# Delta rule on Trainium2: one cyclic list of pieces orders all engines, decay matrices and output weight parts come from the first stage

## The chip, the cores and the metric

The kernel runs on one core of one Trainium2 chip. The metric is the device time of one execution in microseconds (us); the figure for a kernel is the median of its runs. The engines are named as in the profile: PE is TensorE, DVE is VectorE, ACT is ScalarE, POOL is GpSimd, SP is SyncE, which here only issues transfers (DMAs). Each engine works through its own queue in order; a DMA queue on SP or ACT does so too.

## The reference

One inference step of a two-layer encoder over 2048 prompt tokens and 32 sample tokens. Layer one is a gated delta rule with 8 heads of 128, layer two is banded attention. What matters here is the first layer:

```python
def delta_layer(x, conv_buf, s0, w_in, conv_w, a_log, dt_bias, norm_w, w_out, ln_g, ln_b):
    proj = x @ w_in
    qkv, new_buf = causal_conv(proj[..., :CONV_DIM], conv_buf, conv_w)
    z = proj[..., CONV_DIM:CONV_DIM + A_VW].reshape(b, l, A_HEADS, A_DV)
    ...
    o, s_new = gated_delta_rule(q, k, v, g, beta, s0.astype(jnp.float32))
    o = o * lax.rsqrt(jnp.mean(o * o, -1, keepdims=True) + RMS_EPS) * norm_w * jax.nn.silu(z.astype(jnp.float32))
    out = o.reshape(b, l, A_VW).astype(x.dtype) @ w_out
    return layer_norm(DN_ALPHA * x + out, ln_g, ln_b), new_buf, s_new.astype(x.dtype)
```

and within the delta rule, for each chunk of tokens:

```python
    gcum = jnp.cumsum(gb, axis=-1)
    decay = jnp.exp(jnp.where(incl, gcum[..., :, None] - gcum[..., None, :], -jnp.inf))
    lower = jnp.where(strict, jnp.einsum('bhik,bhjk->bhij', kbeta, kc) * decay, 0.0)
    tmat = lower + jnp.eye(c, dtype=lower.dtype)
    ...
    intra = jnp.einsum('bhik,bhjk->bhij', qc, kc) * decay
    def step(s, xs):
        v_new = ui - jnp.einsum('bhck,bhkv->bhcv', wi, s)
        o = jnp.einsum('bhck,bhkv->bhcv', qd, s) + jnp.einsum('bhij,bhjv->bhiv', ai, v_new)
        s = s * gl[..., None, None] + jnp.einsum('bhck,bhcv->bhkv', kd, v_new)
        return s, o
```

The matrix `decay` depends on the gates alone, not on q, k, v or the state.

## The kernel before

All products that have a weight as an operand are made of fp32r parts: a weight or an activation is split into a high and a low part, and three matmuls (high-high, low-high, high-low) stand for one (`project`, lines 73 to 81).

Stage 1 (`P1.qkv`) takes 24 rows of q, k and v; each row is 5 blocks of 416 tokens of 24 matmuls. ACT copies a block from PSUM to the row tile `R` (L227), ACT and DVE do the convolution (L194, L196), the SiLU (L199, L200) and the squares. Ahead of the rows `gates` makes the cumulated log gates and writes one row tile `g_row` per 128 tokens to the DRAM scratch `gcum` (L379 to L382). Through rows 15 to 22 `split_out_weights` (L1031 to L1034) splits the first four of the eight slices of the output weight into parts and stores them in scratch `wo`. Then the gate projection z of the first blocks runs, with the block inverses of the first two chunks beside it (`Ahead`).

The delta stage (`Delta.run`) goes over 17 chunks: chunk 0 is the sample (32 tokens), chunks 1 to 16 have 128 tokens. For a chunk, `decays` adds the causal mask to the broadcast gates (one DVE addition of 128x1024, L542) and takes eight exponentials on ACT (L547); the result is `E`. `powers` takes two more exponentials of the gates (L638). `lower` multiplies k by k (`g`, L562) and then by E (L563); a 25-step chain on POOL (L585, L588) and 6 steps on DVE invert the 32-blocks of the triangle, small matmuls (L680 to L704) join them to 128. `errors` (ks, L714), `changes` (vp, L725), `seen` (op, L739 and L743) and `advance` (sp L755, state Sp L761) are the recurrence; `squares`, `norms`, `scale` (L787) and `emit` (otr L798, L799) are the output norm and gate.

The order of PE, DVE and ACT in this stage is the program's own: `run` advances generators of several chunks in turn by calls of `go`, and between them fills PE from one of two `Filler`s. The first holds 16 blocks of the gate projection (`late_z`) until cycle `OPEN` = 11; the second holds the output projection of finished tiles (po, L1089 to L1091), used from the last cycles on. SP and POOL are ordered by a scheduler. At cycle 11 the output projection's pool is opened; `load_part_weights` (L1036 to L1066) brings in the four split slices and splits the other four from raw: casts on ACT (L1059), subtractions on DVE (L1063), the fetches on the DMA queue of ACT (L1050, L1051), one step at a time as `side(True)` is called.

E has one buffer, the gates `gb` two, k two, q five.

Of the kernel before, what the change touches and what calls it, by code (L numbers as in the profile page):

```python
# [95 lines left out]
class P1:  # L96
# [49 lines left out]
    def qkv(self):  # L146
# [30 lines left out]
        parts = one.tile([128, 8, NT // 32], F32, tag="parts", name="parts")  # L177
        wo = split_out_weights(nc, one, "th", I["a_w_out"], T["wo"])
        for i in range(24):
# [34 lines left out]
        nc.sync.dma_start(self.O["conv"][:, :, :], self.convo[:])  # L214

# [71 lines left out]
    def late_z(self, pool, w, raw):  # L287


        nc = self.nc  # L290
        self.sub = nc.vector
        raws = [raw]

        def last(h, b, p, th):
            z = pool.tile([128, TB], F32, tag="z", name="z")
            nc.vector.tensor_scalar(out=z[:], in0=p[:, :TB], scalar1=self.nwh[:, 0:1], scalar2=None, op0=ALU.mult)
            nc.vector.scalar_tensor_tensor(out=z[:], in0=th[:], scalar=1.0, in1=z[:], op0=ALU.add, op1=ALU.mult)
            self.keep_gate(h, b, z)

        todo = None  # L300
        for h in range(8):
            self.fetched = raws.pop(0) if h < 7 else None
            if h < 6:
                raws.append(self.late_raw(pool, h + 2))
            for b in (3, 4):
                p = self.left_ps()
                for us in project(nc, p[:, :TB], w, self.x[b]):
                    yield us
                    if todo:
                        last(*todo)  # L310
                        todo = None
                th = pool.tile([128, TB], F32, tag="zth", name="zth")
                nc.scalar.activation(th[:], p[:, :TB], AF.Tanh, scale=0.5)
                todo = h, b, p, th
            self.split()
            w = self.next
        yield 0.0
        last(*todo)

# [7 lines left out]
def gates(nc, I, T, G, abT, gtmp, one, pt):  # L327
# [129 lines left out]
class Chunk:  # L457
    def __init__(self, t0, n):
        self.t0, self.n, self.ti, self.ready, self.pool = t0, n, t0 // 128, False, None
        self.split = 25  # L460


class Delta:

    OPEN = 11
    BUFS = 2

# [29 lines left out]
    def constants(self):  # L500
        nc, one = self.nc, self.one
        self.nm = one.tile([128, 128], F32, tag="nm", name="nm")
        nc.sync.dma_start(self.nm[:], self.I["nm"])
        self.tinit = one.tile([128, 32, 8], F32, tag="tinit", name="tinit")
        nc.sync.dma_start(self.tinit[:], self.I["tinit"])

    @staticmethod
    def bc(ap, n, w=128):
        return ap.unsqueeze(2).to_broadcast([n, 4, w])

    def load(self, ch, name, halves=(0, 1)):
        nc, T, n, ti = self.nc, self.T, ch.n, ch.ti
        own = ch.pool is not None and name != "z"
        w = n if own else 128
        if name in ("gb", "k") and 0 in halves:
            if own:
                ch.__dict__[name] = ch.pool.tile([128, 8, w], F32, tag="c" + name, name=name, bufs=1)
            else:
                ch.__dict__[name] = self.four.tile([128, 8, w], F32, tag=name, name=name, bufs=self.BUFS)
        for q in halves:  # L520
            hs = slice(q * 4, q * 4 + 4)
            if name in "vzq":
                src = T[name][ti, :, hs, :n]
# [6 lines left out]
                ch.__dict__.setdefault(name, []).append(t)  # L530
                nc.sync.dma_start(t[:, :, :n], src)
        if name == "gb":
            nc.sync.dma_start(ch.gb[:, :, :n], T["gcum"][ti, :, :n].partition_broadcast(128))
        if name == "k":
            nc.sync.dma_start(ch.k[:, :, :n], T["k"][ti, :, :, :n])

    def decays(self, ch):

        nc, V, G = self.nc, self.nc.vector, self.G
        n, ti = ch.n, ch.ti  # L540
        ch.E = self.two.tile([128, 8, 128], F32, tag="E", name="E", bufs=1)
        V.tensor_tensor(out=ch.E[:n, :, :n], in0=ch.gb[:n, :, :n],  # L542
                        in1=self.nm[:n, :n].unsqueeze(1).to_broadcast([n, 8, n]), op=ALU.add)
        yield
        for h in range(8):
            E = ch.E[:n, h, :n]
            nc.scalar.activation(E, E, AF.Exp, bias=G["ngc"][:n, ti, h:h + 1])  # L547
            if h % 4 == 3:
                yield

    def lower(self, ch):

        nc, V = self.nc, self.nc.vector
        n = ch.n
        ch.npr = self.two.tile([128, 8, 128], F32, tag="npr", name="npr")
        nb = self.sml.tile([128, 8, 32], F32, tag="nb", name="nb")
        for q in range(2):
            hs = slice(q * 4, q * 4 + 4)
            g = self.pa.tile([128, 4, 128], F32, tag="tr", name="g")
            for j in range(4):  # L560
                kt = ch.k[:, q * 4 + j, :n]
                nc.tensor.matmul(g[:n, j, :n], kt, kt, start=True, stop=True)  # L562
            V.tensor_tensor(out=ch.npr[:n, hs, :n], in0=g[:n, :, :n], in1=ch.E[:n, hs, :n], op=ALU.mult)  # L563
            yield
        for b in range(n // 32):
            bs = slice(32 * b, 32 * b + 32)
            nc.scalar.copy(nb[bs], ch.npr[bs, :, bs])
        ch.L = self.two.tile([128, 32, 32], F32, tag="L", name="L")
        ch.Tt = self.keep.tile([128, 32, 8], F32, tag="Tt", name="Tt")
        nc.scalar.copy(ch.Tt[:n], self.tinit[:n])  # L570
        yield
        V.transpose(ch.L[:n], nb[:n].rearrange("q p i -> q i p").unsqueeze(2).to_broadcast([n, 32, 4, 8]))
        yield

    def chain(self, ch, P, a, z):

        if ch.ready:
            return
        n, L, Tt = ch.n, ch.L, ch.Tt
        k = a // 8 * 8  # L580
        tm = self.sml.tile([128, 32 - k, 8], F32, tag="ta" if k else "tm", name="tm")
        for j in range(a, z):
# [4 lines left out]
            yield  # L587
# [3 lines left out]
    def turn_k(self, ch):  # L591
        nc, G, n = self.nc, self.G, ch.n
        ch.kd = []
        for q in range(2):
            kd = self.four.tile([128, 4, 128], F32, tag="kd", name="kd")
            tr = self.pa.tile([128, 4, 128], F32, tag="tr", name="tr")
            for j in range(4):
# [66 lines left out]
    def invert(self, ch):  # L664

        nc, V = self.nc, self.nc.vector
        if ch.n == 32:
            return
# [134 lines left out]
    def run(self, chunks, S, first, second, side, done):  # L803
# [44 lines left out]
        for i in range(len(chunks) + 1):  # L848
# [17 lines left out]
            if last:  # L866
                done(last)
# [997 lines left out]
```

## Time and profile before

| | us |
|---|---|
| median of 3 runs | 2196.88 (2190.58 to 2197.76) |
| the profiled execution | 2196.05 |
| its span | 2194.3 |
| PE busy | 2149.0 |
| DVE busy | 1373.7 |
| ACT busy | 917.6 |
| POOL busy | 841.7 |
| mean granted PE clock | 0.991 of full speed |

A row of a timeline is: start, duration, engine, line, operation, output<-inputs, shape, number of instructions joined in the row, and in brackets how long the engine had been idle before and what released it. A row of the windows is: the stretch, its length, then for each engine busy time and number of instructions, the granted PE clock, the share of the DMA engines that was busy, and GB/s. A group of instructions ends with its busy time and the mean duration of one in ns. Matmuls overlap in the pipeline, so that the duration of one is longer than its share of the time; the distance of starts is what counts. Stage 1 lies at about 0 to 600 us, the z stage and the inverses to about 692, the delta stage to about 1160; the rest is the end of the first layer's projection and the attention layer.

### The profile page before, as it was taken

To read this page: it belongs to the slowest core of one execution; us is meant where nothing else is said; L and a number is where in the kernel's file an instruction comes from. 1 tells how busy PE (TensorE), PEld (TensorE's weight loads), DVE (VectorE), ACT (ScalarE), POOL (GpSimd) and SP (SyncE) were. 2 spreads that over 40 slices of the span, in tenths; PEclk is the share of its full clock that TensorE was granted. 3 is DMA by queue.
4 is the path that set the end of the run, shared out by engine and by line. 5 is a ranking of instruction groups with operands and counts; after the bars stand their busy time and mean duration, and the time that the engine had idled before them with its cause. 6 is when DMAs were issued, how large, how long until landed. Compare 5 with 4: busy or idle time off the path is not lost.

```text
span 2194.3 us, 36636 instructions
## 1 busy us (share of the span) xinstructions
PE 2149.0 (98%) x13706; PEld 1982.3 (90%) x13706; DVE 1373.7 (63%) x2696; ACT 917.6 (42%) x2303; POOL 841.7 (38%) x1189
## 2 busy tenths in 40 slices
PE   8999999999999999999999999999999999999998
PEld 6999999999999899998888788999999987778885
DVE  3676666754466688888868876135442236668775
ACT  4444344433323677778741213222112235445442
POOL 1422212222211377888820201046441124556564
PEclk9999999999999999999999999999999999999999
DMA  5222222233355344446536754374221288233321
GB/s 198 68 60 79 68 78 68 91 117 97 97 152 156 100 139 148 128 134 216 191 98 198 239 186 154 100 235 167 70 76 67 86 181 267 78 96 97 103 67 53
DMA packets 250674, 274.48 MB, mean 125 GB/s; under 512 B 76112, under 2 KB 195216, under 8 KB 250224
## 3 DMA queue, kind: packets, MB, share of 16 engines
q1 hardware_dynamic: 240528, 256.97, 38.0%
q10 hardware_dynamic: 9968, 15.17, 2.1%
q8 instruction: 108, 1.77, 0.3%
q14 instruction: 70, 0.57, 0.1%
HBM read 168.53 MB, written 103.92 MB: 124 GB/s over the span
## 4 chain that ended last, share of the span: by engine, by line
PE 91%; POOL 3%; DMA 2%; DVE 1%; ACT 1%; issue 1%; ACTq 0%; SPq 0%; DVEq 0%; POOLq 0%
PE ps L77 17%; PE ps L79 17%; PE ps L78 17%; PE po L1089 5%; PE po L1091 5%; PE po L1090 5%; PE ot L1581 4%; PE S L1560 2%; PE tr L1575 2%; POOL Tt L588 1%; POOL tm L585 1%; PE g L562 1%; PE vp L725 1%; PE ks L714 1%; PE op L739 1%; PE gq L629 1%
## 5 line engine op out<-in xcount | busy, mean ns | idle before, releaser
L77 PE MATMUL ps<-act_hi,w_hi 128*128 128x416 f32 x2000 | 706.6, 354 | 4.5 <-ACT w_hi L53 3.2
L79 PE MATMUL ps<-act_hi,w_lo 128*128 128x416 f32 x2000 | 704.9, 353 | 2.0 <-POOL w_lo L54 1.2
L78 PE MATMUL ps<-act_lo,w_hi 128*128 128x416 f32 x2000 | 701.6, 351 | 0.0
L77 PEld LDWEIGHTS ps<-act_hi,w_hi 128*128 128x128 f32 x2000 | 377.0, 189 | 9.1 <-ACT w_hi L53 3.7
L79 PEld LDWEIGHTS ps<-act_hi,w_lo 128*128 128x128 f32 x2000 | 376.1, 188 | 6.8 <-POOL w_lo L54 1.7
L78 PEld LDWEIGHTS ps<-act_lo,w_hi 128*128 128x128 f32 x2000 | 376.5, 188 | 4.7 <-DVE act_lo L69 0.4
L54 POOL TENSOR_TENSOR w_lo<-w_raw,w_hi 128x1024 fp32r<-128x1024 f32 x44 | 117.6, 2673 | 469.2 <-ACT w_hi L53 443.1
L196 DVE SCALAR_TENSOR_TENSOR y<-R,convw,y 128x2083 f32<-128x2083 f32 x72 | 173.7, 2414 | 109.6 <-ACT y L194 74.1
L585 POOL TENSOR_TENSOR tm<-L,Tt 128x60 f32<-128x60 f32 (+19 forms) x373 | 139.4, 374 | 89.9 <-ACT vn L771 49.7
L588 POOL TENSOR_TENSOR Tt<-Tt,tm 128x60 f32<-128x60 f32 (+19 forms) x373 | 157.1, 421 | 29.2
L1568 POOL TENSOR_TENSOR P<-P,sm 128x384 f32<-128x384 f32 (+2 forms) x128 | 100.5, 806 | 172.9 <-DVE sm L1446 104.4
L227 ACT COPY R<-ps 128x416 f32<-128x416 f32 (+1 forms) x144 | 61.2, 448 | 199.0 <-PE ps L79 178.4
L1442 ACT ACTIVATE P<-S,nm 128x192 f32<-128x192 f32 (+3 forms) x260 | 104.6, 418 | 90.0 <-DVE nm L1435 43.3
L1089 PE MATMUL po<-wo_hi,g_hi 128*128 128x512 f32 x256 | 104.0, 406 | 1.8 <-ACT hT L1196 1.8
L1286 POOL TENSOR_TENSOR rs<-rs,sin 128x416 f32<-128x416 f32 x50 | 71.0, 1421 | 78.7 <-DVE rs L1285 72.2
L1091 PE MATMUL po<-wo_hi,g_lo 128*128 128x512 f32 x256 | 100.5, 393 | 0.0
L1090 PE MATMUL po<-wo_lo,g_hi 128*128 128x512 f32 x256 | 100.4, 392 | 0.0
L1581 PE MATMUL ot<-pt,vd 128*128 128x256 f32 x372 | 97.1, 387 | 1.6 <-ACT pt L1577 1.1
L53 ACT CAST w_hi<-w_raw 128x1024 fp32r<-128x1024 f32 x48 | 50.4, 1050 | 114.7 <-PE ps L78 87.3
L1089 PE MATMUL po<-wo,g_hi 128*128 128x512 f32 x224 | 92.9, 415 | 0.0
L1091 PE MATMUL po<-wo,g_lo 128*128 128x512 f32 x224 | 90.0, 402 | 0.0
L1090 PE MATMUL po<-wo,g_hi 128*128 128x512 f32 x224 | 89.8, 401 | 0.0
(306 smaller groups left out, 4041.2 us busy)
## 6 DMA issues: line engine op xcount, KB each, us to landing
w_raw<-in_w_in SPq DMA_DIRECT2D x40, 512.0 KB
w_raw<-in_b_w_in SPq DMA_DIRECT2D x20, 512.0 KB
gb<-s_gcum SPq DMA_DIRECT2D x17, 512.0 KB
k<-s_k SPq DMA_DIRECT2D x17, 512.0 KB
s_bz<-za SPq DMA_DIRECT2D x40, 208.0 KB
s_bq<-ra SPq DMA_DIRECT2D x40, 208.0 KB
s_q<-y SPq DMA_DIRECT2D x8, 1024.0 KB
s_k<-y SPq DMA_DIRECT2D x8, 1024.0 KB
```

The costliest lines, as they stand in the source:

```text
L54: sub.tensor_tensor(out=lo[:], in0=raw[:], in1=hi[:], op=ALU.subtract)
L77: nc.tensor.matmul(ps, hi[:, k, :], xh[:, k, :], start=(k == 0), stop=False)
L78: nc.tensor.matmul(ps, hi[:, k, :], xl[:, k, :], start=False, stop=False)
L79: nc.tensor.matmul(ps, lo[:, k, :], xh[:, k, :], start=False, stop=(k == KC - 1))
L196: nc.vector.scalar_tensor_tensor(out=y[:], in0=R[:, j:j + W], scalar=self.convw[:, i, j:j + 1], in1=y[:], op0=ALU.mult, op1=ALU.add)
L585: P.tensor_tensor(out=tm[:n, i0 - k:, :w], in0=L[:n, i0:, j:j + 1].to_broadcast(sh), in1=Tt[:n, j:j + 1, :w].to_broadcast(sh), op=ALU.mult)
L588: P.tensor_tensor(out=Tt[:n, i0:, :w], in0=Tt[:n, i0:, :w], in1=tm[:n, i0 - k:, :w], op=ALU.subtract)
L1089: nc.tensor.matmul(ps[:n], ghi[:, k, :n], w[0][:, k, cs], start=a, stop=False)
L1090: nc.tensor.matmul(ps[:n], ghi[:, k, :n], w[1][:, k, cs], start=False, stop=False)
L1091: nc.tensor.matmul(ps[:n], glo[:, k, :n], w[0][:, k, cs], start=False, stop=z)
L1442: nc.scalar.activation(P[u], src, AF.Exp, bias=nm[:, u:u + 1], scale=1.0, accum_out=sm[:, u:u + 1])
L1581: nc.tensor.matmul(ot[:, p], self.vd[:, kc0 + j, p, :], pt[:, 2 * j:2 * j + 2, :], start=(j == 0), stop=(j == nj - 1))
```

## The change

Four things change.

First, the decay matrices of all chunks are made in stage 1. `gates` also writes the exponentials of the cumulated gates (scratch `grow`), and 34 half tiles of E are made and stored in scratch `E` during rows 16 to 23. The delta stage loads E and grow ready-made.

```diff
+            if i >= 16:
+                for _ in range(5 if i < 18 else 4):
+                    next(matrices)
...
+    def decays(self):
+        nc, G, T = self.nc, self.G, self.T
+        nm = self.one.tile([128, 128], F32, tag="triu", name="nm")
+        nc.sync.dma_start(nm[:], self.I["nm"])
+        todo = [(t, q) for t in (NTT - 1, *range(NTT - 1)) for q in range(2)]
+        def load(m):
+            t, q = todo[m]
+            n, hs = min(128, NT - t * 128), slice(q * 4, q * 4 + 4)
+            E = self.one.tile([128, 4, 128], F32, tag=("parts", "sel", "gtmp")[m % 3], name="E")
+            nc.sync.dma_start(E[:, :, :n], T["gcum"][t, hs, :n].partition_broadcast(128))
+            return E, t, n, hs
+        ahead = [load(0), load(1)]
+        for m in range(len(todo)):
+            E, t, n, hs = ahead.pop(0)
+            if m + 2 < len(todo):
+                ahead.append(load(m + 2))
+            nc.vector.tensor_tensor(out=E[:n, :, :n], in0=E[:n, :, :n],
+                                    in1=nm[:n, :n].unsqueeze(1).to_broadcast([n, 4, n]), op=ALU.add)
+            for j in range(4):
+                h = hs.start + j
+                nc.scalar.activation(E[:n, j, :n], E[:n, j, :n], AF.Exp, bias=G["ngc"][:n, t, h:h + 1])
+            nc.scalar.dma_start(T["E"][t, :n, hs, :n], E[:n, :, :n])
+            yield
...
-        row = one.tile([H, 128], F32, tag="g_row", name="g_row", bufs=2)
-        V.tensor_copy(row[:, :n], tp[:H, :n])
-        nc.scalar.dma_start(T["gcum"][t, :, :n], row[:, :n])
+        row = one.tile([H, 2, 128], F32, tag="g_row", name="g_row", bufs=1)
+        V.tensor_copy(row[:, 0, :n], tp[:H, :n])
+        nc.scalar.activation(row[:, 1, :n], tp[:H, :n], AF.Exp)
+        nc.scalar.dma_start(T["gcum"][t, :, :n], row[:, 0, :n])
+        nc.scalar.dma_start(T["grow"][t, :, :n], row[:, 1, :n])
```

Second, all eight slices of the output weight are split in stage 1 (rows 7 to 22), and the delta stage loads the parts, 16 loads of 512 KB on SP, with no cast or subtraction left.

```diff
-            if 15 <= i < 23:
+            if 7 <= i < 23:
                 next(wo)
...
+def load_whole_weights(nc, pool, kept):
+    hi, lo = (pool.tile([128, KC, D], F32R, tag=n, name=n) for n in ("wo_hi", "wo_lo"))
     yield hi, lo
+    for k in range(KC):
+        nc.sync.dma_start(hi[:, k, :].bitcast(F32), kept[0, k])
+        nc.sync.dma_start(lo[:, k, :].bitcast(F32), kept[1, k])
         yield
```

Third, the order of the delta stage is one cyclic list. A piece `name+off` in cycle i is done for chunk i + off; names stand for the functions of before, cut into pieces for one engine each (G products of k by k, N their weighting, PC0 to PC5 the chain on POOL, T1 to T3 its end on DVE, v1 to v5 the joins, SU the state update, L.. loads, R the root, OSC the scaling, z and st the gating and its store).

```diff
+    OPEN = 11
+    FIRST = -5
+    WHOLE = 2
+    SPLIT = 25
+    ORDER = """
+        ta2+0 fq1+1 os0+0 v5+0 Lk+2 PC2+1 OSC+-1 Lq1+2 PC3+1 fq0+1 vn0+1 G0+2 u3+0 N0+2 G1+2 TT+2 otr0+-1
+        otr1+-1 N1+2 GA1+1 z0+-1 NB+2 tk0+1 tk1+1 vp0+0 vs0+0 PC4+1 kd0+1 st0+-1 z1+-1 Lv1+1 GA3+0 fk+1 L+2
+        PC5+1 kd1+1 vp1+0 Lv0+2 st1+-1 T1+1 oa0+0 T2+1 sp0+0 T3+1 tv1+1 SPR1+1 PC0+2 LE+3 o0+0 vs1+0 SU0+0 gq1+2
+        PC1+2 SPR2+1 os1+0 sp1+0 vn1+1 Lz0+0 oa1+0 SU1+0 sq0+0 at1+2 v1+1 Lgb+2 WH+1 gq0+2 at0+2 o1+0 y1+1 ks0+1
+        e0+1 U32+1 ks1+1 v2+1 v3+1 GA2+1 gth+0 sq1+0 WL+1 X+0 Lz1+0 Lq0+3 ta1+1 v4+1 gz1+0 tv0+2 GA0+2 u1+1 e1+1
+        R+0 gz2+0
+"""
...
+        gate.plan(order, self.FIRST + 2, self.WHOLE)
+        gate.begin()
+        for i in range(self.FIRST, last + 4):
+            if i == self.OPEN:
+                gate.finish()
+                side(None)
+            for p, (name, off) in enumerate(order):
+                c = i + off
+                if name in gate.STEPS:
+                    gate.step(name, c + gate.shift)
+                elif 0 <= c <= last and self.wanted(chunks[c], name):
+                    steps[name](chunks[c])
+                    if i >= last - 1 and name in self.WORK:
+                        second.give(0.45)
+                    if name == "st1":
+                        done(chunks[c])
+                if i >= self.OPEN and p in (len(order) // 3, 2 * len(order) // 3):
+                    side(True)
...
+        for q in range(2):
+            self.back(c0, q)
+            self.gated(c0, q)
+            self.store(c0, q)
+            second.give(2.0)
```

Fourth, the gate blocks of this stage are pieces of the list too (`LateGate`): GA0 to GA3 are a quarter of a block's matmuls each, gth, gz1, gz2 its tanh and weighting, WH and WL the split of the next head's weight; two blocks (WHOLE) are done ahead of the first cycle. `late_z` goes away, the sample chunk's output is gated at the very end, the last chunk's POOL chain has 25 steps as the others (23 before). The loads and buffers become

```diff
-            nc.sync.dma_start(ch.gb[:, :, :n], T["gcum"][ti, :, :n].partition_broadcast(128))
+                t = self.four.tile([128, 8, w], F32, tag=name, name=name, bufs=1 if name == "gb" else self.BUFS)
+            src = T["grow"][ti, :, :n].partition_broadcast(128) if name == "gb" else T["k"][ti, :, :, :n]
+        elif name == "E":
+            ch.E = self.two.tile([128, 8, 128], F32, tag="E", name="E")
+            nc.sync.dma_start(ch.E[:n, :, :n], T["E"][ti, :n, :, :n])
...
-        ch.E = self.two.tile([128, 8, 128], F32, tag="E", name="E", bufs=1)
-        V.tensor_tensor(out=ch.E[:n, :, :n], in0=ch.gb[:n, :, :n],
-                        in1=self.nm[:n, :n].unsqueeze(1).to_broadcast([n, 8, n]), op=ALU.add)
-            nc.scalar.activation(E, E, AF.Exp, bias=G["ngc"][:n, ti, h:h + 1])
```

so that gb has one buffer and E two.

More of the change, by code (lines that the diff above doesn't have):

```diff
@@ L1639, in program @@
     o1 = []
-    def gated():
-        yield from p1.late_z(zp, w, raw)
     def side(o):
@@ L1679, in program @@
     with tc.manual_schedule(engines={ET.PE, ET.DVE, ET.Activation}):
[L1680 removed]
+        delta.run(chunks, S, LateGate(p1, zp, w, raw), second, side, done)
     right.close()
```

754 lines of the change are left out of this document (319 added, 435 removed).

## The prediction

> **What bounds the kernel now.** First the page: span and busy time of each engine.
>
> ```profile
> span 2194.3 us, 36636 instructions
> PE 2149.0 (98%) x13706; PEld 1982.3 (90%) x13706; DVE 1373.7 (63%) x2696; ACT 917.6 (42%) x2303; POOL 841.7 (38%) x1189
> ```
>
> TensorE has work for 98% of the span, so the change can win only where TensorE idles or runs below its full clock, 2194.3 - 2149.0 = 45 us and the dips. The profiled execution took 2196.05 us, 0.83 below the median of the runs (2196.88); I sum against 2196.05. Second the windows of 50 us (after the engines: granted clock, DMA share, GB/s), for where those losses lie.
>
> ```profile
> 550.00:600.00 50.00, 50.00 (x268) 49.68 (x267) 22.68 (x13) 16.43 (x20) 11.54 (x8) 1.00 0.32 98
> 700.00:750.00 50.00, 48.47 (x324) 43.77 (x324) 26.98 (x47) 28.68 (x92) 8.71 (x29) 0.90 0.44 146
> 850.00:900.00 50.00, 50.00 (x546) 47.98 (x545) 42.83 (x102) 39.00 (x124) 39.89 (x101) 1.00 0.45 141
> 1000.00:1050.00 50.00, 44.68 (x533) 41.87 (x535) 42.74 (x109) 40.78 (x128) 41.25 (x108) 1.00 0.68 229
> 1050.00:1100.00 50.00, 46.12 (x542) 44.07 (x538) 42.39 (x100) 40.85 (x127) 42.01 (x103) 0.93 0.49 167
> 1100.00:1150.00 50.00, 46.48 (x370) 41.70 (x368) 31.31 (x86) 19.73 (x58) 10.38 (x19) 0.90 0.32 103
> ```
>
> Three zones. In stage 1 (550) and in the gated part of the delta stage (850) TensorE is never idle: work taken from VectorE or ScalarE there shortens nothing. The prologue (700) loses 1.53 us of idling and 50 x 0.10 = 5 us of clock. From 1000 to 1150, the cycles without gate blocks and the tail, 5.32 + 3.88 + 3.52 us are idle and 3.5 + 5 go to the clock: 21 us, all that the change can reach here. Third, the chunk period: starts of a chunk's G products, in the timeline.
>
> ```profile
> 959.76 2.05 PE L562 MATMUL g<-k 128*128 128x128 f32 x16
> 984.72 2.05 PE L562 MATMUL g<-k 128*128 128x128 f32 x16
> 1008.70 2.05 PE L562 MATMUL g<-k 128*128 128x128 f32 x16
> 1030.65 2.05 PE L562 MATMUL g<-k 128*128 128x128 f32 x16
> 1054.54 2.05 PE L562 MATMUL g<-k 128*128 128x128 f32 x16
> 1078.89 2.05 PE L562 MATMUL g<-k 128*128 128x128 f32 x16
> ```
>
> The gated period is 984.72 - 959.76 = 24.96 us, TensorE full. A gate block in it is 24 matmuls of the kind that fills the window at 550 (50 / 268 = 0.187 each, 4.5 us), so TensorE needs about 20.5 us without it; the open cycles take 21.95, 23.89 and 24.35. What is late there, from the waits on TensorE and its timeline:
>
> ```profile
> PE ks L714 <- DVE Sp L761: 5.9, 4, 2.0
> 1065.76 1.16 PE L714 MATMUL ks<-Sp,k 128*128 128x128 f32 x8 [2.05 <-DVE Sp L761]
> 1067.30 1.91 PE L714 MATMUL ks<-Sp,k 128*128 128x128 f32 x8
> 1040.25 0.20 DVE L585 TENSOR_TENSOR tm<-L,Tt 128x42 f32<-128x42 f32 x1 [1.32 <-POOL Tt L588]
> 1039.93 0.29 POOL L588 TENSOR_TENSOR Tt<-Tt,tm 128x49 f32<-128x49 f32 x1
> ```
>
> The state update waits behind VectorE's last steps of the block inverse, and those wait for GpSimd's 25 steps. That chain is the bound of the open cycles. Its length, and how VectorE stretches it:
>
> ```profile
> 793.48 0.26 POOL L585 TENSOR_TENSOR tm<-L,Tt 128x31 f32<-128x31 f32 x1 [0.85 <-DVE tm L585]
> 804.96 0.36 POOL L588 TENSOR_TENSOR Tt<-Tt,tm 128x68 f32<-128x68 f32 x1
> 805.78 1.18 POOL L588 TENSOR_TENSOR Tt<-Tt,tm 128x64 f32<-128x64 f32 x1
> 816.48 0.29 POOL L588 TENSOR_TENSOR Tt<-Tt,tm 128x49 f32<-128x49 f32 x1
> 805.46 1.32 DVE L542 TENSOR_TENSOR E<-gb,nm 128x1024 f32<-128x1024 f32 x1
> ```
>
> 816.48 + 0.29 - 793.48 = 23.3 us. The step at 805.78 took 1.18 where its neighbour took 0.36, beside the addition that makes E.
>
> **The change, part by part.** (1) Stage 1, +1 us. E is made there, in 34 half tiles: a broadcast load, half an addition, four exponentials, a store. From the rows below that is 34 x 1.31 / 2 = 22 us of VectorE and 136 x 0.389 = 53 us of ScalarE over some 200 us (rows 16 to 23); eight more half steps of the output weight, and 17 exponentials with 17 stores for grow, come to it.
>
> ```profile
> L547 ACT ACTIVATE E<-E,t_ngc 128x128 f32<-128x128 f32 x83 | 25.3, 389 | 0.0
> L542 DVE TENSOR_TENSOR E<-gb,nm 128x1024 f32<-128x1024 f32 x10 | 13.1, 1313 | 0.0
> L638 ACT ACTIVATE gb<-gb 128x512 f32<-128x512 f32 x20 | 11.4, 615 | 0.0
> ```
>
> What hides it is TensorE's own work: the stretch at 550 has VectorE busy for 22.68 and ScalarE for 16.43 of 50. Queued behind these pieces on ScalarE are the evictions of ps; one late by more than its ring of PSUM tiles allows would stop TensorE. Without cover, four exponentials (1.6 us) at 34 places would cost 54; I take 1, with 0 to 10 as ends, since both engines keep half their time.
>
> (2) Prologue and gated cycles, -3.8 us (from -8 to +3). The list runs two gate blocks ahead and lays the rest into every cycle from -3 on. I set the list's pieces against each other by the durations of before: in the gated cycle none waits, so the period stays near 24.96 while VectorE loses 1.3 and ScalarE 8 x 0.389 + 2 x 0.615 = 4.3 us per chunk. The gain is in the prologue: of the 1.53 + 5 lost at 700 I leave 2.7, the sample chunk's small matrices being still there. Full cover wins 6.5, and up to 8 with the waits just at the opening; one stall of the dip's size more loses 3.
>
> (3) Open cycles, -6.1 us before the next point. No E addition and no stretch of 1.18 - 0.36 = 0.8 by it brings the chain to about 22.3, and that is the period while TensorE has 20.5. Before, three periods took 1078.89 - 1008.70 = 70.2, and the fourth open cycle, which has no G, ends with this product:
>
> ```profile
> 1104.64 3.66 PE L725 MATMUL vp<-vn,u 128*128 128x128 f32 x16 [0.91 <-ACT u L705]
> ```
>
> vp follows G by 1.9, so it took 1104.64 - 1.9 - 1078.89 = 23.8, and all four 94.0; after, 3 x 22.3 + 21 (one with no G) = 87.9. [...]
>
> (4) The weight burst, +10.7 us and 2.5 of clock. Before, half the weight came slowly: two raw tiles, one pair, and later pieces paced on ScalarE's queue; its four casts and four subtractions, beside full waits on GpSimd, win nothing that the chain does not already set. After, all 16 loads of 512 KB are on SP's queue. In SP's program order of the changed kernel they all stand, with others, between the last gate stores and the load of k for chunk 14: 16 x 512 of weight, 512 stored g, 512 gb, 256 v, 512 g, 256 q, 1024 r, 512 z, 512 E, 512 ln_g, 512 k itself; 13312 KB = 13.6 MB. The rate of full DMA engines is in the burst that before had at the same place (its issues begin at 1004.74):
>
> ```profile
> 1004.74 0.81 SPq L1047 DMA_DIRECT2D wo_raw<-in_a_w_out  x2
> 1008.00:1012.00 4.00, 4.00 (x43) 3.93 (x41) 2.58 (x4) 4.00 (x14) 3.45 (x8) 1.00 0.99 383
> 1012.00:1016.00 4.00, 4.00 (x38) 4.00 (x38) 3.61 (x6) 3.60 (x11) 3.30 (x10) 1.00 1.05 330
> 1016.00:1020.00 4.00, 3.78 (x34) 3.59 (x34) 4.00 (x16) 2.98 (x17) 2.91 (x10) 1.00 1.02 398
> 872.51 0.32 SPq L535 DMA_DIRECT2D k<-s_k  x1
> 875.00:876.00 1.00, 1.00 (x30) 0.72 (x30) 1.00 (x2) 1.00 (x3) 0.77 (x4) 1.00 0.37 148
> ```
>
> At 383 or the mean of 370 GB/s, 13.6 MB take 35.6 to 36.8 us; at 398, 34.2. The burst opens about 4.0 us ahead of G of chunk 13 (1008.70 - 1004.74), and G of chunk 14 is due a period later, 26.3 us after the burst's start. So k is 8 to 10.5 us late by its bytes. A load of k issued at 872.51, with little beside it, moved its last bytes in the microsecond from 875, about 3 us after its issue, where its bytes need 1.4: some 1.5 more, so 9.5 to 12, and I take 10.7. Behind G of chunk 14 all of TensorE waits, since its queue is in order, and behind TensorE N0, the turn and GpSimd's chain. Ends: 0, if the loads go out in the order in which they are needed or start a cycle earlier, and 12 plus a dip. For a dip after idling:
>
> ```profile
> 1126.56 1.08 PE L686 MATMUL bps<-y,u 64*64 64x64 f32 x15 [2.06 <-ACT y L682]
> 1130.28 2.07 PE L739 MATMUL op<-Sp,q 128*128 128x128 f32 x8
> ```
>
> After 2.06 us of idling eight products took 2.07 where the eight at 1065.76 take 1.16; the dip at 1067.30 follows the wait of 2.05. The clock lost in 1050 to 1150, 8.5 us over four dips, gives 2.1 for one; a longer wait may cost more, 2.5. [...]
>
> (5) Tail, +3 us (from -3 to +7). For chunk 16 the list lays only 0.45 us of output projection behind each piece, 6 matmuls (1.4 us by the kernel's own figure of 0.227 each) between its last output product and otr, where eviction, four squares, twelve small steps and the scaling must go by:
>
> ```profile
> 816.38 0.58 ACT L745 COPY o<-op 128x512 f32<-128x512 f32 x1
> 818.08 0.19 ACT L771 ACTIVATION_READ_ACCUMULATOR vn<-o 128x1 f32 x1
> 804.28 0.23 DVE L436 TENSOR_SCALAR ro_y<-Xo 128x8 int32<-128x8 int32 x1
> 807.90 1.23 DVE L787 TENSOR_TENSOR o<-o,ro_y 128x1024 f32<-128x1024 f32 x1
> ```
>
> Eviction and squares are 818.27 - 816.38 = 1.9. From the first step to the end of the scaling 809.13 - 804.28 = 4.85, less the 1.32 of E's addition that stood in between: 3.5. With one small step more 5.8, so some 4.4 idle, and a dip of 2.1. A layer norm of nineteen instructions stands on VectorE ahead of z1 of chunk 15 and of both last state updates: 1.5 more. The wait at 1126.56 stays with part of its dip, 3. That makes 11, where before lost 3.52 + 5 in the window of 1100, of which I count 8 to this part.
>
> The sum: 1 - 3.8 - 6.1 + 10.7 + 2.5 + 3 = +7.3, so 2196.05 + 7.3 = 2203.4; I say 2204, rounded towards the unproven exposures of a fixed order.
>
> **The rivals.** Burst hidden (faster): k of chunk 14 lands before it is needed, because the loads start a cycle earlier or because their transfers overlap better than in before. For it: at 1012 TensorE was whole under a full DMA. Against it: one queue and 13.6 MB. Time: 2196.05 + 1 - 3.8 - 6.1 + 1 for the tail = 2188. The list exposes a wait in each cycle (slower): every piece is at a fixed place with no cover for its latencies; if ks after SU1, or gq after its eviction, comes 0.9 us late in each of 14 chunks, that is +12.6 on the forecast: 2216. Against it: the same pieces ran at 850 without a wait; it decides from about 0.5 us per cycle. Nothing much (the list reproduces the old order and the loads are harmless): 2197.
>
> **How the numbers follow.** Forecast 0.47, own range 2193 to 2213 by the ends of (2) and (4). Hidden burst 0.28, exposed waits 0.18, nothing much 0.07. Within 0.3% (6.6 us, about what a measurement tells) means 2190.3 to 2203.5. The forecast gives 0.02 faster, 0.18 same, 0.27 slower; the hidden burst 0.23 and 0.05; the exposed waits 0.18 slower; the last 0.02, 0.04, 0.01. Together 0.27 faster, 0.27 same, 0.46 slower. The range, 2186 to 2217, takes in both neighbours' values and leaves out some 0.2.
>
> **What would show it.** Right: a wait of about 10 us of a g product (L627 of the changed kernel) for k's load one cycle after the opening, DMA share near 1.0 for over 30 us, G periods near 25.0 before and 22.3 after it, a wait of otr in the last chunk. Wrong: G of chunk 14 on time, a gated period off 25.0 by over 0.3, or TensorE below 50.00 in the windows from 300 to 650.

## The result and the profile after

The changed kernel takes 2219.09 us (median of 4 runs, 2216.86 to 2222.18), before 2195.8 (the runs shown with it): a ratio of 1.0111, 95% interval 1.0089 to 1.0133. It is slower by 1.1%, outside the range of 2186 to 2217. The profiled execution took 2216.86, 20.8 more than that of before. The page first:

```profile
span 2215.1 us, 36944 instructions
PE 2150.1 (97%) x13690; PEld 1980.3 (89%) x13690; DVE 1379.1 (62%) x2701; ACT 901.1 (41%) x2274; POOL 826.3 (37%) x1201
```

TensorE is busy for the same 2150 us; nearly the whole loss, 19.7 us of the 20.8 in the span, is time in which it stands. Where, say the windows of the changed kernel (columns as before), the last line from the kernel before:

```profile
550.00:600.00 50.00, 45.52 (x226) 44.06 (x225) 27.24 (x17) 27.19 (x58) 11.11 (x10) 0.93 0.68 200
600.00:650.00 50.00, 48.22 (x258) 46.79 (x258) 28.02 (x40) 15.10 (x23) 11.02 (x6) 0.97 0.63 171
700.00:750.00 50.00, 49.81 (x323) 46.67 (x322) 28.14 (x54) 16.59 (x45) 5.75 (x19) 1.00 0.53 171
850.00:900.00 50.00, 50.00 (x544) 48.09 (x543) 40.42 (x99) 32.69 (x104) 36.51 (x100) 1.00 0.46 154
1000.00:1050.00 50.00, 34.02 (x423) 32.39 (x421) 30.06 (x80) 25.10 (x85) 33.52 (x94) 0.86 0.88 328
1150.00:1200.00 50.00, 44.39 (x223) 36.37 (x221) 33.65 (x92) 11.24 (x29) 4.79 (x2) 0.93 0.53 168
...
600.00:650.00 50.00, 50.00 (x278) 49.16 (x277) 29.19 (x75) 11.53 (x26) 7.63 (x3) 1.00 0.58 159
```

New holes lie at the end of stage 1 (550 to 650), which was whole before, and in the tail (1150 to 1200, busy for 49.33 before); the hole after the opening (1000 to 1050) has grown from 5.3 to 16 us. The prologue (700) has lost its hole and its dip, the gated cycles are whole as before. The timeline of the G products and the list of TensorE's waits from 990 to 1200 (total, times, longest), changed kernel:

```profile
966.40 2.05 PE L627 MATMUL g<-k 128*128 128x128 f32 x16
990.44 2.05 PE L627 MATMUL g<-k 128*128 128x128 f32 x16
1011.86 2.05 PE L627 MATMUL g<-k 128*128 128x128 f32 x16
1052.33 3.76 PE L627 MATMUL g<-k 128*128 128x128 f32 x16 [12.16 <-DMA k<-s_k]
1074.52 2.05 PE L627 MATMUL g<-k 128*128 128x128 f32 x16
1095.96 2.05 PE L627 MATMUL g<-k 128*128 128x128 f32 x16
```

```profile
PE g L627 <- DMA k<-s_k: 12.2, 1, 12.2
PE vtr L741 <- DMA v<-s_v: 6.2, 1, 6.2
PE otr L848 <- DVE o L839: 4.3, 1, 4.3
```

The G products of chunks 13 and 16 start at 1011.86 and 1095.96, before at 1008.70 and 1078.89. One more landmark is needed, the last of the 24 z products of the z stage on VectorE, first in before, then in the changed kernel:

```profile
692.69 0.65 DVE L241 TENSOR_SCALAR z<-ps,nwh 128x416 f32<-128x416 f32 x1 [1.44 <-ACT zth L240]
```

```profile
705.79 0.64 DVE L272 TENSOR_SCALAR z<-ps,nwh 128x416 f32<-128x416 f32 x1
```

With these three marks the 20.8 us split up (after less before, each mark less the one ahead of it):

| stretch | forecast | measured |
|---|---|---|
| to the end of the z stage: step (1) | +1 | 705.79 - 692.69 = +13.1 |
| to G of chunk 13: step (2) | -3.8 | 3.2 - 13.1 = -9.9 |
| to G of chunk 16: step (3) for three periods, and (4) | 66.9 - 70.2 + 13.2 = +9.9 | 17.1 - 3.2 = +13.9 |
| to the end: step (3) for the fourth open cycle, and (5) | 21 - 23.8 + 3 = +0.2 | 20.8 - 17.1 = +3.7 |

**The burst.** Issues on SP in the changed kernel, and a window of 4 us from the stretch:

```profile
1012.25 1.04 SPq L1045 DMA_DIRECT2D wo_hi<-s_wo  x1
...
1043.21 0.32 SPq L598 DMA_DIRECT2D k<-s_k  x1
```

```profile
1044.00:1048.00 4.00, 0.00 (x0) 0.00 (x0) 0.00 (x0) 0.00 (x0) 0.00 (x0) 0.50 1.03 409
```

SP issues the load of k 31 us after the first of the weight, and it is used another 9.1 us later. About half of the 31 us is due to the queue: the buffer of k came free only at 1027, when the products ks of chunk 12 had read it. From 1028 to 1048 the DMA engines move 403 to 413 GB/s, and from 1044 to 1048 no engine works at all: the core waits for the end of 13.6 MB in one queue, of which it wants the last 512 KB.

**Stage 1.** The end of stage 1 in the changed kernel, ScalarE and then all waits of TensorE from 400 to 710:

```profile
574.34 1.87 ACTq L244 DMA_DIRECT2D s_E<-E  x2
581.61 0.62 ACT L1034 CAST wo_parts<-wo_parts 128x512 fp32r<-128x512 f32 x1 [6.84 <-DMA s_E<-E]
582.13 1.04 ACT L53 CAST w_hi<-w_raw 128x1024 fp32r<-128x1024 f32 x1
583.08 0.56 ACT L258 COPY R<-ps 128x384 f32<-128x384 f32 x2
```

```profile
PE ps L77 <- ACT R L258: 2.4, 1, 2.4
PE ps L79 <- POOL w_lo L54: 2.1, 1, 2.1
PE ps L79 <- POOL w_lo L301: 1.8, 1, 1.8
```

ScalarE is idle for 6.84 us in front of a cast of the output weight's split (L1034). Behind that cast stand the next weight's cast (L53), from which GpSimd makes the low part w_lo (L54), and the eviction of ps (L258); TensorE waits for both. The third wait is for the low part of a weight of the z stage. The three are 6.3 us, and the clock in the windows of 550 and 600 takes 3.5 + 1.5 more. It looks as if the output weight's split were the culprit; the third experiment tests that.

### The profile page after: what moved, and what is told of

It is laid out like the page before. It is cut to its first block, busy times and chain, and to the rows that moved or that the text cites. A ratio compares the mean times of both kernels' runs of the same rounds, so it can differ in the third digit from the quotient of the medians.

```text
span 2215.1 us, 36944 instructions
## 1 busy us (share of the span) xinstructions
PE 2150.1 (97%) x13690; PEld 1980.3 (89%) x13690; DVE 1379.1 (62%) x2701; ACT 901.1 (41%) x2274; POOL 826.3 (37%) x1201
## 4 chain that ended last, share of the span: by engine, by line
PE 83%; DMA 7%; DVE 4%; POOL 2%; ACT 2%; issue 1%; SPq 0%; ACTq 0%; DVEq 0%; POOLq 0%
PE ps L77 14%; PE ps L79 14%; PE ps L78 14%; PE po L1070 5%; PE po L1072 5%; PE po L1071 5%; PE ot L1562 4%; DMA E<-s_gcum 2%; PE S L1541 2%; PE tr L1556 2%; DMA s_E<-E 1%; PE g L627 1%; PE gq L754 1%; PE sp L769 1%; PE ks L769 1%
## 5 line engine op out<-in xcount | busy, mean ns | idle before, releaser
L54 POOL TENSOR_TENSOR w_lo<-w_raw,w_hi 128x1024 fp32r<-128x1024 f32 x44 | 117.7, 2675 | 473.4 <-ACT w_hi L53 446.2
L200 DVE SCALAR_TENSOR_TENSOR y<-R,convw,y 128x2083 f32<-128x2083 f32 x72 | 181.8, 2526 | 38.7 <-POOL convo L194 22.5
L661 POOL TENSOR_TENSOR tm<-L,Tt 128x60 f32<-128x60 f32 (+19 forms) x375 | 130.3, 347 | 116.6 <-DVE tm L661 48.0
L663 POOL TENSOR_TENSOR Tt<-Tt,tm 128x60 f32<-128x60 f32 (+19 forms) x375 | 143.8, 383 | 29.4
L258 ACT COPY R<-ps 128x416 f32<-128x416 f32 (+1 forms) x144 | 60.7, 444 | 123.8 <-PE ps L79 105.3
L53 ACT CAST w_hi<-w_raw 128x1024 fp32r<-128x1024 f32 x48 | 50.4, 1050 | 119.5 <-PE ps L78 82.7
L1070 PE MATMUL po<-wo,g_hi 128*128 128x512 f32 x224 | 92.9, 415 | 0.0
L1352 DVE SCALAR_TENSOR_TENSOR za<-zs,za 128x416 f32<-128x416 f32 x40 | 33.0, 826 | 93.3 <-ACT za L1351 93.2
```

The source lines that it names most:

```text
L54: sub.tensor_tensor(out=lo[:], in0=raw[:], in1=hi[:], op=ALU.subtract)
L200: nc.vector.scalar_tensor_tensor(out=y[:], in0=R[:, j:j + W], scalar=self.convw[:, i, j:j + 1], in1=y[:], op0=ALU.mult, op1=ALU.add)
L661: P.tensor_tensor(out=tm[:n, i0 - k:, :w], in0=L[:n, i0:, j:j + 1].to_broadcast(sh), in1=Tt[:n, j:j + 1, :w].to_broadcast(sh), op=ALU.mult)
L663: P.tensor_tensor(out=Tt[:n, i0:, :w], in0=Tt[:n, i0:, :w], in1=tm[:n, i0 - k:, :w], op=ALU.subtract)
L1070: nc.tensor.matmul(ps[:n], ghi[:, k, :n], w[0][:, k, cs], start=a, stop=False)
```

## The experiments

All times are medians; the ratio is to before, run on the same chip, where before came to between 2193.6 and 2195.8. Differences to the changed kernel carry that spread.

**The weight's loads paced on ScalarE's queue** (e1_wo_paced).

```diff
-        nc.sync.dma_start(hi[:, k, :].bitcast(F32), kept[0, k])
-        nc.sync.dma_start(lo[:, k, :].bitcast(F32), kept[1, k])
+        nc.scalar.dma_start(hi[:, k, :].bitcast(F32), kept[0, k])
+        nc.scalar.dma_start(lo[:, k, :].bitcast(F32), kept[1, k])
         yield
```

> The changed kernel with one edit: the 16 loads of the output weight's parts are issued on ScalarE's DMA queue, a pair at each of the eight side steps of cycles 11 to 14, instead of on SP's queue. Theory (order in one queue): the waits of 6.15 us for v of chunk 13 and 12.16 us for k of chunk 14 and the half clock around them (about 4 us) go, some 22 us less than the changed kernel's 2219: 2195 to 2199; the G periods of all open cycles come to 21 to 22 us. Rival (the bytes themselves are too many for these cycles, whatever queue carries them): waits for v, k or E stay at 8 us or more together, and under 12 us are won.

Measured: 2201.47 (ratio 1.0027, 1.0016 to 1.0037), 17.6 less than the changed kernel. Its waits on TensorE from 990 to 1200:

```profile
PE g L627 <- DMA k<-s_k: 2.6, 2, 2.1
...
PE vtr L741 <- DMA v<-s_v: 2.0, 1, 2.0
```

18.3 us of waits became 4.6. That the loads, as they stand on SP's queue, make the waits is shown; the time is 2.5 above what I expected, and 4.6 us of the waits stay. Here k and the weight go at different times, so order and density are not yet separated.

**The same loads on ScalarE's queue, all at the opening** (e2_wo_burst_act): as above, with no `yield` between the pairs.

```diff
     for k in range(KC):
-        nc.sync.dma_start(hi[:, k, :].bitcast(F32), kept[0, k])
-        nc.sync.dma_start(lo[:, k, :].bitcast(F32), kept[1, k])
+        nc.scalar.dma_start(hi[:, k, :].bitcast(F32), kept[0, k])
+        nc.scalar.dma_start(lo[:, k, :].bitcast(F32), kept[1, k])
+    for k in range(KC):
         yield
```

> The changed kernel with one edit: the same 16 loads go to ScalarE's DMA queue, but all at the opening, not paced. The traffic is as dense as in the changed kernel, only k, v and the rest do not stand behind it. Theory (order in one queue): SP's own 5.2 MB up to k share the engines half and half with the weight, some 26 us, so that k of chunk 14 is at most 0 to 5 us late: 14 to 22 us less than 2219, 2197 to 2205. Rival (density of traffic, not the order): waits for v and k together stay above 12 us, and the time above 2211.

Measured: 2222.76 (1.0119, 1.0101 to 1.0137), no gain, and yet neither theory was right. Its wait list and ScalarE's timeline:

```profile
PE gq L754 <- ACT kd L748: 22.5, 1, 22.5
```

```profile
1017.78 0.33 ACTq L1045 DMA_DIRECT2D wo_hi<-s_wo  x1
...
1042.16 1.14 ACT L748 ACTIVATE kd<-ktr,t_ekd 128x128 f32<-128x128 f32 x4 [22.64 <-DMA wo_hi<-s_wo]
```

No wait for k or v is left, but that does not prove the theory of order: TensorE itself stood for 22.5 us, and SP issued k of chunk 14 at 1052.43, behind the last load of the weight (1041.79). That the two queues share the engines half and half was my estimate and is not shown. Order and density stay unseparated. What the run shows is that ScalarE's own instructions stand behind its 16 issues, which go out over 24 us (1017.78 to 1041.79): it idled for 22.64. In the changed kernel SP took 23 us for the same 16 (1012.25 to 1035.42) and held back transfers alone; here ScalarE held back its own work too. The wait changed its place and lost nothing of its length.

**The weight's split ahead of E's rows** (e3_wo_early).

```diff
-            if 7 <= i < 23:
+            if i < 16:
                 next(wo)
```

> The changed kernel with one edit: the 16 half steps that split the output weight run in rows 0 to 15 of stage 1 instead of rows 7 to 22, so that none shares a row with the E pieces. Theory (in the last rows a cast of the weight split stands on ScalarE waiting for its load, which is late behind E's transfers, and the eviction of ps stands behind the cast): the idle times of TensorE between 575 and 610 us and the half clock after them go, 8 to 13 us less than 2219: 2206 to 2211. Rival (E's own transfers and its work on ScalarE and VectorE stop the rows): TensorE still idles 3 us or more there, and under 4 us are won.

Measured: 2220.46 (1.0105, 1.0083 to 1.0128): nothing won in sum, but the sum hides two effects. A mark between them is ScalarE's first convolution step (L198) of row 15, the last row without E pieces, in the changed kernel and then in this one; the last line is the end of this one's z stage:

```profile
399.88 2.04 ACT L198 ACTIVATE y<-R,convw 128x2083 f32<-128x2083 f32 x1
...
407.53 2.04 ACT L198 ACTIVATE y<-R,convw 128x2083 f32<-128x2083 f32 x1
...
708.45 0.64 DVE L272 TENSOR_SCALAR z<-ps,nwh 128x416 f32<-128x416 f32 x1
```

Up to the mark this kernel is 7.65 us late. Its new place brought a new stall, in row 2, again a cast that waits for its load with evictions behind it (ScalarE, then TensorE):

```profile
108.07 0.62 ACT L1034 CAST wo_parts<-wo_parts 128x512 fp32r<-128x512 f32 x1 [4.56 <-DMA wo_parts<-in_a_w_out]
...
109.15 0.72 PE L77 MATMUL ps<-act_hi,w_hi 128*128 128x416 f32 x1 [5.25 <-ACT R L258]
```

From the mark to the end of the z stage it takes 300.9 us, the changed kernel 305.9 and before 293.0 (from 399.71). So of the 12.9 us that these rows lose, 5.0 go with the weight's split and 7.9 stay. VectorE and TensorE at the end of stage 1:

```profile
577.74 0.69 DVE L239 TENSOR_TENSOR E<-E,nm 128x512 f32<-128x512 f32 x1 [2.44 <-DMA E<-s_gcum]
...
584.31 0.46 PE L77 MATMUL ps<-act_hi,w_hi 128*128 128x416 f32 x1 [4.25 <-ACT R L258]
```

With the weight's cast gone a part of the same thing happens by E's own pieces: the addition waits 2.44 us for E's load, the exponentials wait for the addition, and the eviction behind them lets TensorE stand for 4.25. The gain in these rows, 5.0, is less than the theory's 8 to 13 and more than the rival's 4: the weight's split and E's pieces both have a share.

**More output projection ahead of the last otr** (e4_tail).

```diff
+                    if name == "otr0" and c == last:
+                        second.give(6.0)
                     steps[name](chunks[c])
```

> The changed kernel with one edit: 6 us of output projection are laid in front of the last chunk's first otr, and so later work comes earlier. Theory: the wait of 4.28 us of that otr for the scaling on VectorE goes, 3 to 5 us less than 2219: 2214 to 2216. Rival (the wait only moves to the next chunk tile, since the output projection itself waits for the last chunk): under 1.5 us won.

Measured: 2208.84 (1.0059, 1.0042 to 1.0076), 10.3 less, twice what I expected. The wait of 4.28 is gone, but the output projection now waits at two places for its residual r, so that little is won there, much as the rival said. The larger gain lies later. In the changed kernel TensorE waits at the start of the second layer, eight times from 1371 to 1395, for the split of its activations, 5.7 us together. The new wait in this run, then the longest of the eight in the changed kernel:

```profile
PE po L1072 <- DVE r L1080: 3.1, 2, 2.8
...
1384.66 0.45 PE L78 MATMUL ps<-act_lo,w_hi 128*128 128x416 f32 x1 [1.93 <-DVE act_lo L69]
```

With the fill 0.6 of the 5.7 is left. That an earlier output projection brings the second layer's activations earlier is the likely link; it was not tested by itself.

**E made in the delta stage** (e5_E_delta). One part of the change is undone: no E pieces in stage 1; E is loaded as broadcast gates and made at the list's end.

```diff
-            if i >= 16:
-                for _ in range(5 if i < 18 else 4):
-                    next(matrices)
...
-            nc.sync.dma_start(ch.E[:n, :, :n], T["E"][ti, :n, :, :n])
+            nc.sync.dma_start(ch.E[:n, :, :n], T["gcum"][ti, :, :n].partition_broadcast(n))
...
+    def masked(self, ch):
+        n = ch.n
+        self.nc.vector.tensor_tensor(out=ch.E[:n, :, :n], in0=ch.E[:n, :, :n],
+                                     in1=self.nm[:n, :n].unsqueeze(1).to_broadcast([n, 8, n]), op=ALU.add)
+
+    def powers(self, ch, q):
+        n = ch.n
+        for h in range(4 * q, 4 * q + 4):
+            E = ch.E[:n, h, :n]
+            self.nc.scalar.activation(E, E, AF.Exp, bias=self.G["ngc"][:n, ch.ti, h:h + 1])
...
-        R+0 gz2+0
+        DA+3 DX0+3 R+0 gz2+0 DX1+3
```

> The changed kernel with one part undone: E is not made in stage 1 but in the delta stage, from the broadcast gates, with an addition (DA) and two pieces of four exponentials (DX0, DX1) for chunk i + 3 at the end of the list; weight, gates and order stay as changed. Theory (E's own pieces and transfers stop stage 1): the last z of the z stage, at 705.8 us in the changed kernel and 692.7 before, comes to 693 to 695, the gated period stays within 0.2 us of 25.16 since TensorE bounds it, the open period rises from 21.4 to about 22.3 by GpSimd's stretched chain; 8 to 12 us less than 2219: 2207 to 2211. Rival (the sixteen half steps of the weight or the second gate row stop stage 1): the z stage still ends at 701 or later. Second rival (the ready-made E is what keeps the list free of waits): the gated period rises above 25.6 and the gain is under 4 us.

Measured: 2211.83 (1.0079, 1.0065 to 1.0092), 7.3 less. Its z stage, and an open period:

```profile
694.79 0.64 DVE L268 TENSOR_SCALAR z<-ps,nwh 128x416 f32<-128x416 f32 x1
```

```profile
1065.51 3.67 PE L636 MATMUL g<-k 128*128 128x128 f32 x16
1089.48 3.64 PE L636 MATMUL g<-k 128*128 128x128 f32 x16
```

Stage 1 gets back 705.79 - 694.79 = 11.0 us: without E's pieces TensorE has no wait in its last rows, and the weight's split and the second gate row together cost at most 694.79 - 692.69 = 2.1. Of this 5.4 are lost again before G of chunk 13 (311.4 us from the end of the z stage, 306.1 in the changed kernel), 2.8 of them in the prologue and the rest in the two periods just before that G. The gated period stays at 25.16. But the open period is 23.97, not 22.3, and the G products take 3.6 instead of 2.05.

**The three edits together** (e6_all), e5 with e1 and e4.

> Three edits together: E in the delta stage, the weight's loads paced on ScalarE's queue, 6 us of output projection ahead of the last otr. If the three costs (stage 1, queue order, tail) are separate, their gains add: 2219 less 17.6, less 10.3, less the 8 to 12 expected of E: 2179 to 2183, faster than before by 12 to 16. If they overlap (the open cycles bounded by GpSimd again hide what pacing wins), 2186 or more.

Measured: 2189.51 (0.9981, 0.9972 to 0.9990): faster than before, but 6.5 above the upper end of the sum. ScalarE and TensorE in an open cycle:

```profile
1049.35 2.45 ACT L629 ACTIVATE E<-E,t_ngc 128x128 f32<-128x128 f32 x8
```

```profile
1052.46 1.16 PE L742 MATMUL u2p<-u,ta 64*64 64x64 f32 x16 [1.93 <-ACT ta L737]
```

Eight exponentials stand ahead of an eviction (ta, L737) that TensorE waits for, 1.93 us in each of four cycles, and each wait is followed by G products of some 3.6 us. The open period of 23.98 is this wait and its dip: in these cycles TensorE has no wait for the block inverse, the end of GpSimd's chain.

**The weight's pairs at earlier pieces** (e7_all_early): the side steps at pieces 16 and 45 of the list, counted from 0.

```diff
-                if i >= self.OPEN and p in (len(order) // 3, 2 * len(order) // 3):
+                if i >= self.OPEN and p in (16, 45):
```

> As the three edits together, with the weight's pairs issued at the 17th and 46th piece of the list instead of the 31st and 61st, so that none is in flight when k is loaded. Theory (the 2.6 us for k and 2.0 us for v that were left with paced loads come from a pair in flight ahead of k): those waits go, 3 to 5 us less than the kernel of the three edits. Rival (they come from the other loads of the opening, q, g, r and ln_g, on SP's queue): no difference beyond 1.5 us.

Measured: 2191.01 (0.9980, 0.9971 to 0.9989), no difference. It decides nothing: e6 has no wait for k or v in its list, so with open cycles of 24 us the waits that it was to remove had gone already.

**E's pieces earlier in the list** (e8_E_earlier), here against the kernel of the three edits (e6).

```diff
-        otr1+-1 N1+2 GA1+1 ... PC0+2 LE+3 o0+0 vs1+0 SU0+0 ... SU1+0 sq0+0 at1+2
+        otr1+-1 N1+2 LE+3 GA1+1 ... PC0+2 DA+3 o0+0 vs1+0 DX0+3 SU0+0 ... SU1+0 sq0+0 DX1+3 at1+2
-        DA+3 DX0+3 R+0 gz2+0 DX1+3
+        R+0 gz2+0
```

> The kernel of the three edits, with the pieces that make E (LE, DA, DX0, DX1 for chunk i + 3) moved from the list's end to its first half and middle, so that none stands on ScalarE ahead of ta2. Theory (the open cycles of the three edits last 23.98 us because u2p waits 1.9 us in each for ta2, behind four exponentials, and the half clock follows each wait): the waits go, the open period comes to 21.5 to 22.5, 6 to 10 us less than 2189.5: 2180 to 2184. Rival (GpSimd's chain, stretched again by E's addition, bounds the open cycles): the period stays at 23 or more and under 4 us are won.

Measured: 2223.55 (1.0145, 1.0126 to 1.0165), 34 more, from moving four pieces. A miss, and the clearest lesson on the list. Its waits from 700 to 990, in the gated cycles that had had none:

```profile
PE tp L715 <- ACT u L697: 15.4, 8, 2.5
PE gq L763 <- ACT vn L757: 6.3, 8, 0.8
```

The gated period rises from 25.16 to 27.7 and more. ScalarE is busy for 32.7 of 50 us there; it has the time, but not at that place: the exponentials now stand ahead of vn (L757) and U32 (L697), whose readers come soon.

**Half of E in stage 1** (e11_hybrid), with the paced loads and the fill ahead of otr as in e6: ready-made for chunks 0 to 3 and 13 to 16, two half tiles a row instead of four or five, the others in the list at the places of the last run.

```diff
+            if i >= 16:
+                next(matrices)
+                next(matrices)
-        todo = [(t, q) for t in (NTT - 1, *range(NTT - 1)) for q in range(2)]
+        todo = [(t, q) for t in (NTT - 1, 0, 1, 2, 12, 13, 14, 15) for q in range(2)]
```

> As the kernel with E's pieces earlier in the list, but E of chunks 0 to 3 and 13 to 16 comes ready-made from stage 1 (16 half tiles, two in each of rows 16 to 23, instead of 34) and only chunks 4 to 12, which the gated cycles prepare, make it in the list. Theory (stage 1 is stopped by the density of E's pieces: with two for a row ScalarE's evictions no longer stand behind a late load, and the open cycles want E ready-made): TensorE stays whole to the end of the z stage (last z of line 272's kind by 693 to 695), the open period 21 to 22: 2176 to 2182, faster than before by 13 us or more. Rival (any E piece in the last rows stops them, since the eviction stands behind it): the z stage ends 5 us or more later than before, 2184 or more.

Measured: 2212.59 (1.0080, 1.0064 to 1.0097), too slow by 30 for the places in the list, which waits as in the last run. On stage 1 the answer is clear:

```profile
694.26 0.65 DVE L272 TENSOR_SCALAR z<-ps,nwh 128x416 f32<-128x416 f32 x1
```

With 16 pieces the stage ends 1.6 us later than before, with none (e5) 2.1, with 34 13.1: 16 in these eight rows cost nothing that can be seen, and it is 34 that stop them. Whether 34 spread over more rows would pass was not tried.

**The same with the pieces back at the list's end** (e12_hybrid_end).

> As the hybrid, with the pieces that make E of chunks 4 to 12 put back to the list's end, where the kernel of the three edits had them and its gated cycles lasted 25.16 us with no wait; the open cycles have no such piece. If the parts are separate, it adds up: z stage ends at 694.3 as in the hybrid, from there to the G of chunk 13 306 us as in the changed kernel (1000.4), to the G of chunk 16 69 as with paced loads, 1111 to 1112 to the end: a span of 2181, 2179 to 2185 us, faster than before by 9 to 15. If the position was not the cause of the waits in the gated cycles, they last 27 us or more again and the time is above 2200.

Measured: 2182.57 (0.9951, 0.9937 to 0.9964), 12 us faster than before and 36.5 faster than the change; span 2179.2 against 2181 expected. Its gated period, then G of chunk 13 and of chunk 16:

```profile
906.30 2.05 PE L641 MATMUL g<-k 128*128 128x128 f32 x16
931.46 2.05 PE L641 MATMUL g<-k 128*128 128x128 f32 x16
...
1002.63 2.05 PE L641 MATMUL g<-k 128*128 128x128 f32 x16
...
1071.12 2.05 PE L641 MATMUL g<-k 128*128 128x128 f32 x16
```

25.16 again, and 68.5 for the three open periods, where before took 70.2 and the change 84.1. So the change is a gain once its two costs, the E pieces in stage 1 and the loads on SP's queue, are cut down and the tail is filled. The list by itself, without the ready-made E and weight parts, was not run.

## Why the prediction was wrong

**Step (1), stage 1, is the one that failed.** It said +1 with ends of 0 and 10, "since both engines keep half their time". The measured cost is 13.1. One of its own signs of being wrong came about: TensorE below 50.00 between 300 and 650 (45.52 and 48.22). Busy shares do not answer the question: on ScalarE the eviction of ps stands behind exponentials, these wait for an addition, and this for a load into one of only three buffers; in e3 the addition waited 2.44 us for its load, and TensorE 4.25 for the eviction. The prediction named the eviction as what is queued behind and then priced it by idle time; the low parts of the weights, for which TensorE waited 3.9 of its 6.3 us, it did not name. Undoing E alone gives back 11.0 (e5), halving the number of its pieces 11.5 (e11). The weight's split has a share: moved away, it leaves these rows 5.0 better (e3), though without E it costs at most 2.1 (e5). The two do not add: E's pieces without the split lose 7.9, the split without E's pieces at most 2.1, both together 12.9. What makes the loads late is known in part. SP's waits from 500 to 605 in the changed kernel have this as the largest:

```profile
SPq L231 <- DMA s_E<-E: 34.2, 15, 6.9
```

The load of E waits 15 times for the store of an earlier E that frees one of the three buffers, and what SP issues next stands behind it. Whether more buffers or less traffic beside them would cure it was not tried.

**Step (4) was right in mechanism and too small.** k came after G was due, as worked out, and TensorE stood 12.16 us for it against 10.7 forecast. The agreement is partly luck. The burst opened 0.4 us behind G of chunk 13 (1012.25 against 1011.86), not 4.0 ahead of it as taken over from before, and v of chunk 13 in the same queue made TensorE stand 6.15 us first, which put off the moment when k was due. I had summed the bytes up to k only, not those up to v. The waits are 18.3 together. Over the three periods the term is 84.1 - 3 x 21.44 = 19.8, against 10.7 + 2.5. That the loads on SP's queue made the waits is shown by e1, which leaves 4.6 of the 18.3. Whether it was their order in the queue or their density stays open, since e2 did not separate them.

**Step (3), the open cycles**, was right in sign and modest: 21.44 (1074.52 to 1095.96), not 22.3. TensorE needs about 20.5 of it and waits 1.02 us for the end of the block inverse (y1p for tcp), so the chain still bounds the period, but by less than I made it.

**Step (2), prologue and gated cycles**: -9.9 against -3.8. The prologue's idle time and dip went nearly altogether (49.81 and clock 1.00 at 700). Not all of it comes from there: the two periods before G of chunk 13 are 3.5 shorter (45.5 against 48.9), the last of them 21.42, as short as an open one, since two gate blocks are done ahead of the first cycle. The list also leaves some pieces of the next chunk behind G that were ahead of it before; how much this moves the mark was not measured. The gated period was right, 25.16 against 24.96, with no wait above 0.2 us.

**Step (5), the tail**: +3.7 against +0.2 with the fourth open cycle. The wait of otr was right, 4.28 against 4.4. The waits at the second layer's start, 5.7 in all, were not foreseen. They are more than the whole error of 3.5, so other terms of this step came out smaller than priced.

**The rivals.** The measured time is nearest to that of the exposed waits (2216), but its cause is not there: the gated cycles of the change have no wait. With its own pieces the list exposes nothing there; e8 shows what four pieces at bad places do. The hidden burst is refuted. The errors of (1), +12.1, and of (2), -6.1, have opposite signs; with +4.0 of (3) and (4) up to G of chunk 16 and +3.5 behind it they make the 13.5 by which the sum missed the profiled execution.

## What to carry to other kernels

Price work that is put under a busy engine by what is queued behind it on its own engine and by the latency of what it waits for, not by that engine's idle share: 53 us of exponentials laid under a ScalarE that was half idle cost 11 us, and half as many cost nothing that can be seen. The two loads on ScalarE did not add here (at most 2.1 and 7.9 us alone, 12.9 together), so try each in the presence of the other. When an experiment moves work, look at the place where it arrives too: in e3 a gain of 5.0 us was hidden by a loss of 7.65 at the new place. When loads are gathered in one queue, list the bytes ahead of every later load, not of one, and count from where the burst really opens; moving them all at once to an engine that also computes moved the wait there (22.5 us of TensorE in e2). A fixed list can be tested piece by piece: the same four pieces were free at its end in gated cycles (25.16 us a period in e5 and e12), cost 1.9 us and a dip a cycle there in open ones, and 2.5 us and more in its middle.

## What the runs showed of the hardware

The issuing engine stood behind its own transfers: in e2 sixteen issues on ScalarE's queue took 24 us for their 8.4 MB, and ScalarE was idle for 22.64 us before the activation behind them. In the changed kernel the DMA engines held 403 to 413 GB/s from 1028 to 1048, above the mean of 370 that I had taken from the shorter burst of before. Products ran slower after some short waits again, but not after all: in e6 four waits of 1.93 to 1.94 us were each followed by G products of 3.58 to 3.68 us where 2.05 is usual, in e5 two of three such waits by 3.67 and 3.64; after the first of e5, of 1.93 us at 1005.15, G took 2.05, and after one of 1.83 us in the kernel before, at 1041.65, eight products took the usual 1.16. In the long stall of the changed kernel the granted clock was 0.50 from 1044 to 1056.
